# Seven products of quarters for 19 of the 22 up pairs in both gated MLPs of a three-layer fp32 kernel

## The chip, the cores and the metric

One NeuronCore of a Trainium2 chip. The metric is the device time of one execution in microseconds. Three runs of the kernel before gave 1880.21, 1881.07 and 1881.81 us; the median is 1881.07 us.

## The reference, cut to what matters

The network has one block of a first type (pooling, stick-breaking attention, a plain MLP) and then two layers of a second type. The change lies in the gated MLP at the end of each second-type layer:

```python
h2 = _rmsnorm(x, g_ffn[l])                       # x: 512 positions x 1024
z = _dwconv(h2 @ w_up[l], w_dw_ffn[l], b_dw_ffn[l])   # w_up: 1024 x 5632, conv of 3 taps along the positions
zg, zv = jnp.split(z, 2, axis=-1)                # 2816 gate and 2816 value channels
x = x + (jax.nn.silu(zg) * zv) @ w_down[l]       # w_down: 2816 x 1024
```

Everything is float32, and the last layer is followed by one more rmsnorm.

## The kernel before, in words

Channels lie on partitions and the 512 positions on the free axis, so the stream `x` is eight tiles of 128x512. A product with weights takes a 128x128 block of weights as the stationary side and 512 positions as the moving side. To keep float32 accuracy each operand is split into a high and a low part (`fp32r`), and `mm3` (L378) issues three matmuls for a block: high with high (L380), high weights with low data (L381), low weights with high data (L382).

Weights come in units of up to eight blocks, in the order of use that `weight_plan` writes down. `prep` (L352) handles a unit: SP loads `raw` (L358, 512 KB, three buffers), ACT casts it to `whi` (L359), POOL subtracts to get `wlo` (L360); `whi` and `wlo` have four buffers each. `take` (L363) hands out one block after the other and prepares units up to three ahead of the one in use. SP, ACT and POOL work their queues in order; a scheduler laid the order down when the program was built.

The gated MLP of layer `l` is the last part of `layer2`. `norm_in` scales and splits `x` into `xh` and `xl` and sums squares into `acc`; `fin` (`finish` in `norm_in`) makes the factor `r` from them by a matmul with ones (`total`, L480) and `rsqrt`. As `r` is one number for each position it is applied after the product: first `proj_outer` computes four tiles (two pairs of gate and value) with `x`'s eight tiles in the outer loop, then `fin` runs, then come the other pairs, one tile after the other. A pair is a gate tile and a value tile of 128 channels; 22 pairs make the layer. Of each tile `conv3` multiplies by `r` (L1289, DVE), applies the middle tap (L1292, ACT) and the outer taps (L1293 and L1294, DVE); `silu` (L344), the product with the value (L1308) and `split` (L448 and L449) follow. After eleven pairs comes a chunk of `w_down`: eight output tiles of eleven blocks each, added to `x` (L1313). There are two such chunks in a layer. At the very end `final` computes the last two output tiles in halves of 256 positions, so that the norm and the outputs of the first half can run beside the second.

PSUM has eight banks here, all under the name `b`.

Of the kernel before, what the change touches and what calls it, by code (L numbers as in the profile page):

```python
# [21 lines left out]
P = 128  # L22
# [21 lines left out]
NCV = 4  # L44
FF2 = 2816
NF2 = FF2 // P
CHUNK2 = 11
GLU_EARLY = 3
NYB = 7
YBANKS = ("s", "s", "t", "t", "av")  # L50
# [25 lines left out]

def _span(c0, n=P):
    return np.arange(c0, c0 + n)


def weight_plan():
# [47 lines left out]
    for l in range(NL):  # L129
        cr = QL + KVL  # L130
        ca, cg = cr + ROPE, cr + ROPE + 512
        add(outer("w_in_2", l, KT, [_span(ca), _span(cg), _span(ca + P), _span(cg + P)]))
        for i in range(2, GLU_EARLY):
            add(tiles("w_in_2", l, k8, _span(ca + P * i)))
            add(tiles("w_in_2", l, k8, _span(cg + P * i)))
        add(tiles("w_in_2", l, k8, np.concatenate([cr + np.arange(32)] * 2 + [cr + perm] * 2)))
        for j in range(2):
            add(tiles("w_in_2", l, k8, _span(QL + P * j)))
        for j in range(3):
            add(tiles("w_in_2", l, k8, _span(P * j)))  # L140
# [20 lines left out]
        for c in range(NF2 // CHUNK2):  # L161
            fs = list(range(c * CHUNK2, (c + 1) * CHUNK2))
            if c == 0:
                add(outer("w_up_2", l, KT, [_span(P * f + o) for f in fs[:2] for o in (0, FF2)]))
                fs = fs[2:]
            for f in fs:
                add(tiles("w_up_2", l, k8, _span(P * f)))
                add(tiles("w_up_2", l, k8, _span(FF2 + P * f)))
            add([("w_down_2", l, P * k, _span(P * m)) for m in range(KT) for k in range(c * CHUNK2, (c + 1) * CHUNK2)])
    return units  # L170


def pack_weights(inputs, plan):
    out = np.zeros((len(plan), P, UNIT * P), np.float32)
    for u, blocks in enumerate(plan):
        for b, (name, l, r0, cols) in enumerate(blocks):
            w = inputs[name] if l is None else inputs[name][l]
# [4 lines left out]
    return out  # L182

# [66 lines left out]


class Kern:
    def __init__(self, tc, xT, w, vec, cst, pos, outT):
        self.tc, self.nc = tc, tc.nc
        self.xT, self.w, self.vec_d, self.cst_d, self.pos_d, self.outT = xT, w, vec, cst, pos, outT
        self.plan = weight_plan()
        self.units = {}
        self.prepped = 0  # L260
        self.cur, self.blk = 0, 0
        self.table, self.table_users = None, []
# [2 lines left out]
    def setup(self, ctx):  # L265
# [2 lines left out]
        pool = lambda name, bufs=1, **k: ctx.enter_context(tc.tile_pool(name=name, bufs=bufs, **k))  # L268
        self.const = pool("const")
        self.wp = pool("wp", 4, reuse_waits="tile")  # L270
        self.xp = pool("xp", KT, reuse_waits="tile")
        self.rp = pool("rp", 2, reuse_waits="tile")
        c = self.const
# [13 lines left out]
        self.tk = c.tile([P, S], F32, name="tk")  # L287
        self.epst = c.tile([P, 1], F32, name="epst")
        nc.gpsimd.memset(self.epst, EPS)
        self.lna = {}  # L290
        for n in (D, 512, QL, KVL):
            t = c.tile([P, 1], F32, name=f"lna{n}")
# [54 lines left out]
        return ins  # L347


    def prep(self, u, eng=None):  # L350
        nc = self.nc
        n = len(self.plan[u]) * P  # L352
        raw = self.wp.tile([P, UNIT * P], F32, name="raw", bufs=3)
        hi = self.wp.tile([P, UNIT * P], FR, name="whi")
        lo = self.wp.tile([P, UNIT * P], FR, name="wlo")
        cuts = (0, n) if eng is None else (0, n // 2, n)
        for cs in map(slice, cuts, cuts[1:]):
            nc.sync.dma_start(out=raw[:, cs], in_=self.w[u, :, cs])  # L358
            nc.scalar.copy(out=hi[:, cs], in_=raw[:, cs])  # L359
            (eng or nc.gpsimd).tensor_tensor(out=lo[:, cs], in0=raw[:, cs], in1=hi[:, cs].bitcast(F32), op=ALU.subtract)  # L360
        self.units[u] = (hi, lo)

    def take(self, n=1, ahead=AHEAD):  # L363
# [38 lines left out]
    def proj_outer(self, pool, tag, acts, n, parts=WHOLE, between=None):  # L402
# [90 lines left out]
    def norm_in(self, pool, gname, l, on_pool=KT - 2):  # L493
# [14 lines left out]
        def finish(pp, tag):  # L508
            r = self.rp.tile([P, S], F32, name="r", bufs=1)
            self.rsqrt(r, self.total(pp, tag, acc)[0], D)  # L510
            return r

        return acts, split, finish

# [467 lines left out]
    def layer2(self, l, carry=None):  # L982
# [299 lines left out]
        xgp = xg.__enter__()  # L1282
        acts, split_in, fin = self.norm_in(xgp, "g_ffn_2", l)
        split_in()
        ffc = tc.tile_pool(name="ffc", bufs=CHUNK2, reuse_waits="tile")
        fp = ffc.__enter__()

        def conv3(ps, f, tag):
            V.tensor_tensor(out=ps, in0=ps, in1=r, op=ALU.mult)  # L1289
            w3 = self.v("w_dw_ffn_2", l, 3 * f, 3)  # L1290
# [6 lines left out]
        for c in range(NF2 // CHUNK2):  # L1297
            a = []
            pss = []
            if c == 0:  # L1300
                pss = self.proj_outer(pp, "b", acts, 4)
                r = fin(pp, "b")
            for f in range(c * CHUNK2, (c + 1) * CHUNK2):
                pg, pv = pss[2 * f : 2 * f + 2] if 2 * f < len(pss) else (self.proj(pp, "b", acts), self.proj(pp, "b", acts))
                cg = conv3(pg, f, "cg")
                cv = conv3(pv, NF2 + f, "cv")
                self.act(AF.Silu, out=cg, in_=cg)
                V.tensor_tensor(out=cg, in0=cg, in1=cv, op=ALU.mult)  # L1308
                a.append(self.split(fp, cg, ("ah", "al")))
            tail = 2 if l == NL - 1 and c == NF2 // CHUNK2 - 1 else 0  # L1310
            for m in range(KT - tail):
                ps = self.proj(pp, "b", a)
                V.tensor_tensor(out=self.x[m], in0=self.x[m], in1=ps, op=ALU.add)  # L1313
            if tail:
                self.final(pp, a)
        self._close(ffc)
        self._close(xg)
        self._close(pp_)

    def final(self, pp, a):  # L1320

# [14 lines left out]

        def half(j, ps, cs):
            i = KT - 2 + j
            V.tensor_tensor(out=self.x[i][:, cs], in0=self.x[i][:, cs], in1=ps, op=ALU.add)
            gain(i, cs, cs.start == 0 or j == 0)  # L1340

        def norm(cs):
            self.rsqrt(r[:, cs], self.total(pp, "b", acc[:, cs], *late)[0], D)
            late.clear()
            for j in range(0, KT, OUT_TILES):
                o = op.tile([P, OUT_TILES, S // 2], F32, name="o")
                for i in range(OUT_TILES):
                    (G if j + i in OUT_POOL else V).tensor_tensor(out=o[:, i, :], in0=self.x[j + i][:, cs], in1=r[:, cs], op=ALU.mult)
# [7 lines left out]
            norm(HALVES[1])  # L1356


def program(tc, xT, w, vec, cst, pos, outT):
    from contextlib import ExitStack  # L1360

    with ExitStack() as ctx:
        k = Kern(tc, xT, w, vec, cst, pos, outT)
        k.setup(ctx)
        carry = k.block1()
        for l in range(NL):
            k.layer2(l, carry)
# [3 lines left out]
def arrays(inputs):  # L1371
    inputs = {n: np.asarray(a) for n, a in inputs.items()}
    return {
        "xT": np.ascontiguousarray(inputs["x"][0].T),
        "w": pack_weights(inputs, weight_plan()),
        "vec": pack_vectors(inputs),
        "cst": shape_constants(),
        "pos": np.ascontiguousarray(inputs["positions_2"]),
# [12 lines left out]
```

## Time and profile before

| | |
|---|---|
| median of 3 runs | 1881.07 us |
| profiled execution, its own time | 1880.29 us |
| its span, first to last instruction | 1878.6 us |
| PE busy | 1839.2 us (98%) |
| POOL, ACT, DVE busy | 50%, 50%, 51% |
| mean granted TensorE clock | 0.998 of full speed |
| DMA traffic | 164.89 MB, mean 88 GB/s |

Times in the views are microseconds from the span's start. The matmuls are pipelined: the duration of one row overlaps the next, so the price of a matmul is the distance between two starts. PEld is the load of weights, which runs beside the matmuls.

### The profile page before, as it was taken

The numbers are of one execution on the slowest core, as the hardware profiler recorded it, in microseconds if no ns is written. First come the engines' busy times: TensorE is split into PE (matmuls) and PEld (weight loads), VectorE is DVE, ScalarE is ACT, GpSimd is POOL, SyncE is SP. The second block draws the span as 40 slices with busy tenths as digits, with TensorE's granted clock in tenths as the row PEclk, the third lists the DMA queues.
The fourth block names the chain that finished last, engine by engine and source line by source line (L and its number), as shares of the span: only waits on it lengthen the run. The fifth ranks groups of instructions, "written<-read, shape, count | busy, mean of one in ns | idle before, by whom it ended". The sixth has DMA issues, their size and how long they took to land.

```text
span 1878.6 us, 22097 instructions
## 1 busy us (share of the span) xinstructions
PE 1839.2 (98%) x8448; PEld 1495.8 (80%) x8448; DVE 958.1 (51%) x1420; ACT 946.3 (50%) x1442; POOL 938.4 (50%) x510
## 2 busy tenths in 40 slices
PE   8999999999999999999999999999999999999997
PEld 6877888888888888766888888888866788888886
DVE  4666552724022037997565225522898565405543
ACT  6766633643243347697554224433778554314442
POOL 5233444644444557866644444454966464444442
PEclk9999999999999999999999999999999999999999
DMA  5111223222222222200222222222210122222221
GB/s 188 68 57 62 79 101 135 93 94 101 92 99 98 94 90 71 98 29 21 94 106 95 97 101 91 101 101 90 91 51 23 64 99 101 101 91 101 100 91 56
DMA packets 48649, 164.89 MB, mean 88 GB/s; under 512 B 5536, under 2 KB 7584, under 8 KB 48544
## 3 DMA queue, kind: packets, MB, share of 16 engines
q1 hardware_dynamic: 46304, 160.34, 24.3%
q10 hardware_dynamic: 2240, 3.15, 0.5%
q8 instruction: 66, 1.08, 0.2%
q14 instruction: 39, 0.32, 0.1%
HBM read 161.37 MB, written 2.10 MB: 87 GB/s over the span
## 4 chain that ended last, share of the span: by engine, by line
PE 89%; DVE 6%; ACT 3%; issue 1%; POOL 1%; DMA 0%; SPq 0%; DVEq 0%; ACTq 0%; POOLq 0%
PE b L381 23%; PE b L382 23%; PE b L380 23%; PE mm L381 3%; PE s L1140 3%; PE mm L380 3%; PE mm L382 3%; PE t L1157 2%; DVE xl L452 1%; PE av L1162 1%; PE av L1163 1%; PE cv L480 1%; ACT whi L359 1%; DVE x L650 1%; PE b L480 1%
## 5 line engine op out<-in xcount | busy, mean ns | idle before, releaser
L360 POOL TENSOR_TENSOR wlo<-raw,whi 128x1024 fp32r<-128x1024 f32 x300 | 720.9, 2405 | 809.9 <-ACT whi L359 809.6
L359 ACT CAST whi<-raw 128x1024 fp32r<-128x1024 f32 (+1 forms) x302 | 313.6, 1040 | 506.4 <-PE b L381 414.6
L380 PE MATMUL b<-xh,whi 128*128 128x512 f32 (+1 forms) x1296 | 495.4, 382 | 2.7 <-ACT xh L451 2.7
L381 PE MATMUL b<-xl,whi 128*128 128x512 f32 (+1 forms) x1296 | 491.4, 379 | 3.4 <-DVE xl L452 3.4
L382 PE MATMUL b<-xh,wlo 128*128 128x512 f32 (+1 forms) x1296 | 491.1, 379 | 0.0
L381 PEld LDWEIGHTS b<-xl,whi 128*128 128x128 f32 x1296 | 244.1, 188 | 51.9 <-DVE xl L452 4.2
L380 PEld LDWEIGHTS b<-xh,whi 128*128 128x128 f32 x1296 | 244.2, 188 | 50.5 <-ACT xh L451 3.1
L382 PEld LDWEIGHTS b<-xh,wlo 128*128 128x128 f32 x1296 | 244.1, 188 | 45.6
L380 PE MATMUL b<-ah,whi 128*128 128x512 f32 (+1 forms) x646 | 243.6, 377 | 0.0
L381 PE MATMUL b<-al,whi 128*128 128x512 f32 (+1 forms) x646 | 243.2, 377 | 0.0
L382 PE MATMUL b<-ah,wlo 128*128 128x512 f32 (+1 forms) x646 | 243.2, 376 | 0.0
L381 PEld LDWEIGHTS b<-al,whi 128*128 128x128 f32 x646 | 121.6, 188 | 22.4
L380 PEld LDWEIGHTS b<-ah,whi 128*128 128x128 f32 x646 | 121.5, 188 | 22.4
L382 PEld LDWEIGHTS b<-ah,wlo 128*128 128x128 f32 x646 | 121.6, 188 | 22.0
L1228 POOL TENSOR_TENSOR cacc<-cacc,pd 128x510 f32<-128x510 f32 (+14 forms) x94 | 119.8, 1275 | 26.6 <-ACT pd L1226 22.8
L1212 DVE SCALAR_TENSOR_TENSOR cv<-u,vec,cv 128x497 f32<-128x497 f32 (+13 forms) x146 | 108.2, 741 | 8.4 <-ACT cv L1202 6.5
L1289 DVE TENSOR_TENSOR b<-b,r 128x512 f32<-128x512 f32 x88 | 61.0, 697 | 97.3 <-PE b L382 97.1
L1313 DVE TENSOR_TENSOR x<-x,b 128x512 f32<-128x512 f32 x30 | 20.6, 687 | 161.3 <-PE b L382 161.3
L448 ACT CAST ah<-cg 128x512 fp32r<-128x512 f32 x44 | 27.3, 621 | 98.7 <-DVE cg L1308 98.7
L380 PE MATMUL mm<-xh,whi 128*128 128x512 f32 x176 | 69.3, 394 | 0.0
L871 DVE TENSOR_TENSOR b<-rl,b 128x512 f32<-128x512 f32 x32 | 22.1, 696 | 92.5 <-ACT rl L870 92.5
L381 PE MATMUL mm<-xl,whi 128*128 128x512 f32 x176 | 68.7, 391 | 0.0
(430 smaller groups left out, 2851.0 us busy)
## 6 DMA issues: line engine op xcount, KB each, us to landing
raw<-w SPq DMA_DIRECT2D x295, 512.0 KB, 3.2
x<-xT SPq DMA_DIRECT2D x8, 256.0 KB, 6.5
x<-xT ACTq DMA_DIRECT2D x8, 256.0 KB, 4.8
raw<-w SPq DMA_DIRECT2D x7, 256.0 KB, 2.6
outT<-o ACTq DMA_DIRECT2D x4, 256.0 KB, 2.4
outT<-o SPq DMA_DIRECT2D x4, 256.0 KB, 2.5
vec<-vec SPq DMA_DIRECT2D x1, 363.0 KB, 6.9
f<-pos SPq DMA_DIRECT2D x1, 256.0 KB, 3.3
```

Of the source, the lines that this page charges most:

```text
L359: nc.scalar.copy(out=hi[:, cs], in_=raw[:, cs])
L360: (eng or nc.gpsimd).tensor_tensor(out=lo[:, cs], in0=raw[:, cs], in1=hi[:, cs].bitcast(F32), op=ALU.subtract)
L380: mm(ps, lhsT=wb[0], rhs=xb[0], start=start, stop=False, **kw)
L381: mm(ps, lhsT=wb[0], rhs=xb[1], start=False, stop=False, **kw)
L382: mm(ps, lhsT=wb[1], rhs=xb[0], start=False, stop=stop, **kw)
L448: nc.scalar.copy(out=hi, in_=src)
L480: self.nc.tensor.matmul(full[:, :n], lhsT=self.ones, rhs=a, start=i == 0, stop=i == len(parts) - 1)
L1140: mm(s, lhsT=q[:, qb * P : (qb + 1) * P], rhs=k, start=True, stop=True)
L1157: nc.tensor.transpose(pt[:, qb * P : (qb + 1) * P], probs[qb][:, t * P : (t + 1) * P], self.ident)
L1212: ins = V.scalar_tensor_tensor(out=acc[:, o], in0=us[i][:, u], scalar=self.v("w_dw_conv_2", l, i * CONV_K + k), in1=acc[:, o], op0=ALU.mul ...
L1228: G.tensor_tensor(out=acc[:, o], in0=acc[:, o], in1=pd, op=ALU.add)
L1289: V.tensor_tensor(out=ps, in0=ps, in1=r, op=ALU.mult)
```

## The change

19 of the 22 pairs of each layer (`PLAIN2 = 3` stay as they were) are computed as a product of 2x2 quarters with seven multiplications in place of eight. The weights of a pair are cut into gate and value, and into the lower and upper half of the 1024 inputs (`a11`, `a12`, `a21`, `a22`, each four blocks); the data into the lower and upper half of the inputs and the left and right 256 positions (`B11`, `B21`, `B22` and four sums `T1` to `T4`). The seven products take the stationary sides `a11`, `a12`, `a22` and four sums of quarters, `S1` to `S4`. Each product is four blocks by 256 positions, three matmuls a block.

The sums of weights are made on the chip, in DRAM: `sums` lists for each layer 20 copies (issued on ACT's queue) and 20 accumulating transfers (issued on POOL's queue), each over up to four pairs (1 MB). `prep` issues one of these 80 behind every second weight unit from unit 26 on, with none between units 106 and 140: layer 0's 40 stand behind units 26 to 104 (the first block), layer 1's behind units 142 to 220 (the gated MLP of layer 0, units 141 to 235). `quarter_inputs` makes the seven data operands, high and low, from `x` and the norm's factor; therefore `fin` now stands inside `proj_outer`, behind its third step of eight. In these MLPs raw weights have five buffers and are loaded five units ahead. The down products come in three chunks (7, 7 and 8 pairs), the first three tiles of each with the pairs in the outer loop. In `final` the outputs of the first half are issued after the second half's factor, some of them behind the second half's last addition.

```diff
-CHUNK2 = 11
+CHUNKS2 = (0, 7, 14, 22)
+PLAIN2 = 3
+OUTER2 = 2
+NDOWN = 3
+SUM_PAIRS = 4
+SIDE = {u: 1 for u in range(26, 240, 2) if not 105 < u < 141}
+RAW2, LOAD_AHEAD2 = 5, 5
...
+        for _ in range(SIDE.get(u, 0)):
+            if self.side:
+                begin, on_pool = self.side.popleft()
+                self.issue_behind(begin(), rest if on_pool else cast)
...
+        def copy(dst, src):
+            return lambda: nc.scalar.dma_start(out=dst, in_=src)
+        def add(dst, src):
+            return lambda: nc.gpsimd.dma_start(out=dst, in_=src, accum_op=ALU.add, max_dma_last_dim=row)
...
+        for name, base, more in (("S1", "a21", "a22"), ("S3", "a11", "a21"), ("S2", "S1", "a11"), ("S4", "S2", "a12")):
...
+            stages += [(copies, "S1", l), [(adds, "S1", l), (copies, "S3", l)], [(adds, "S3", l), (copies, "S2", l)], (adds, "S2", l), (copies, "S4", l), (adds, "S4", l)]
...
+        while self.loaded < min(self.cur + 1 + self.load_ahead, len(self.plan)):
+            self.load(self.loaded)
...
             for k, a in enumerate(acts):
+                if k == OUTER_LAG + 2 and between is not None:
+                    between()
...
+                def snap(ps):
+                    t = fp.tile([P, S // 2], F32, name="snap", bufs=4)
+                    with tc.high_priority():
+                        A.copy(out=t, in_=ps)
+                    return t
+                def plus(out, a, b):
+                    with tc.high_priority():
+                        V.tensor_tensor(out=out, in0=a, in1=b, op=ALU.add)
+                def times(ps, name, start, stop):
+                    hi, lo = ops[name]
+                    for kk in range(KT // 2):
+                        self.mm3(ps, self.take(), (hi[:, kk], lo[:, kk]), start and kk == 0, stop and kk == KT // 2 - 1, skip_group_check=True)
+                def p4(g):
+                    times(g["v"][:, L], "T4", False, True)
+                    plus(g["v"][:, R], g["g"][:, R], g["u3"])
+                def p3(g):
+                    times(g["g"][:, R], "B22", False, True)
+                    plus(g["g"][:, R], g["g"][:, R], g["u2"])
+                    a.append(unit(g["f"], g["g"], g["v"], self.wneg[l][:, 3 * g["f"] : 3 * g["f"] + 3]))
...
+                    times(g["v"][:, L], "B11", True, False)
+                    u1 = snap(g["v"][:, L])
+                    times(g["g"][:, L], "B21", True, True)
+                    plus(g["g"][:, L], g["g"][:, L], u1)
+                    if old is not None:
+                        p4(old)
+                    times(g["v"][:, L], "T2", False, False)
+                    g["u2"] = snap(g["v"][:, L])
+                    times(g["g"][:, R], "T1", False, False)
+                    if old is not None:
+                        p3(old)
+                    times(g["v"][:, L], "T3", False, False)
+                    g["u3"] = snap(g["v"][:, L])
+                    old = g
```

How the instructions stand now. PE at the start of layer 0's MLP (`b` numbered 7975 to 7978 are the first four tiles, `whi`/`wlo` the weights, `ones` the matrix of the norm's total); before, the total stood behind the last of the 96 matmuls of `proj_outer`:

```order
L507 MATMUL b_7978<-xh_7902,whi_7826 128x512
L508 MATMUL b_7978<-xl_7903,whi_7826 128x512
L509 MATMUL b_7978<-xh_7902,wlo_7827 128x512
L609 MATMUL b_8034<-acc_7897,ones_115 128x512
L507 MATMUL b_7975<-xh_7904,whi_7826 128x512
L508 MATMUL b_7975<-xl_7905,whi_7826 128x512
```

The total (L609) now stands behind 36 of these matmuls, with 60 behind it.

ACT in layer 0, in the second chunk of pairs (`snap` holds a copy of a half bank, `cv`, `cg` and `ah` belong to the pair that is being finished, `S2` is a sum in DRAM). Before, two casts and four other operations made a pair:

```order
L421 CAST whi_9209<-raw_9135 128x1024
L1472 COPY snap_9225<-b_9156 128x256
L1442 ACTIVATE cv_9264<-b_9065,vec_67,wneg0_124 128x512
L421 CAST whi_9242<-raw_9172 128x1024
L1442 ACTIVATE cg_9260<-b_9066,vec_67 128x512
L1472 COPY snap_9286<-b_9156 128x256
L421 CAST whi_9293<-raw_9206 128x1024
L1472 COPY snap_9309<-b_9288 128x256
L390 ACTIVATE b_9066<-cg_9260 128x512
L421 CAST whi_9327<-raw_9239 128x1024
L577 CAST ah_9270<-b_9066 128x512
L464 DMA S2_1_1_163<-S1_1_1_162 16x16384
```

Snaps, casts of weights and the finishing of a pair alternate now, and a copy in DRAM stands between them.

POOL in the same chunk, where before it had only the `wlo` of each unit:

```order
L467 DMA S3_1_0_160<-wq 512x512
L422 TENSOR_TENSOR wlo_9139<-raw_9067,whi_9138 128x1024
L422 TENSOR_TENSOR wlo_9176<-raw_9101,whi_9175 128x1024
L422 TENSOR_TENSOR wlo_9210<-raw_9135,whi_9209 128x1024
```

One accumulating transfer stands in this queue for every four units here; where the transfers of `S2` and `S4` are issued it is one for every two.

## Rows read from the trace of the kernel before

**Rows 1.** The page: chain that ended last, by engine.
```profile
PE 89%; DVE 6%; ACT 3%; issue 1%; POOL 1%; DMA 0%; SPq 0%; DVEq 0%; ACTq 0%; POOLq 0%
```
**Rows 2.** Busy time by stretch (engine: us busy, instructions; clock, DMA share, GB/s).
```profile
10.00:13.00 3.00, 3.00 (x15) 2.47 (x14) 0.97 (x2) 3.00 (x6) 1.98 (x1) 1.00 1.04 403
946.00:1062.00 116.00, 116.00 (x513) 95.84 (x512) 66.91 (x93) 53.79 (x69) 50.73 (x22) 1.00 0.28 96
```
**Rows 3.** PE in order of time (start, duration), down products, 512 positions wide.
```profile
1845.72 0.39 PE L382 MATMUL b<-ah,wlo 128*128 128x512 f32 x1
...
1850.48 0.39 PE L382 MATMUL b<-ah,wlo 128*128 128x512 f32 x1
```
**Rows 4.** The same right behind, 256 positions wide.
```profile
1850.71 0.28 PE L380 MATMUL b<-ah,whi 128*128 128x256 f32 x1
...
1859.58 0.28 PE L382 MATMUL b<-ah,wlo 128*128 128x256 f32 x1
```
**Rows 5.** Start of layer 0's MLP in order of time (PE, DVE, ACT, DVE).
```profile
923.73 0.39 PE L380 MATMUL b<-xh,whi 128*128 128x512 f32 x1
...
932.00 0.68 DVE L463 TENSOR_TENSOR acc<-acc,sq 128x512 f32<-128x512 f32 x1
...
946.55 0.69 ACT L344 ACTIVATE r<-b,epst 128x512 f32<-128x512 f32 x1
...
949.50 0.69 DVE L491 SCALAR_TENSOR_TENSOR r<-b,r 128x512 f32<-128x512 f32 x1
```
**Rows 6.** Groups by line, 946 to 1062 us: busy us, mean ns | idle before, releaser.
```profile
L360 POOL TENSOR_TENSOR wlo<-raw,whi 128x1024 fp32r<-128x1024 f32 x22 | 52.9, 2404 | 67.7 <-ACT whi L359 67.7
...
L359 ACT CAST whi<-raw 128x1024 fp32r<-128x1024 f32 x22 | 23.1, 1052 | 27.4 <-PE b L381 27.3
...
L1292 ACT ACTIVATE cg<-b,vec 128x512 f32<-128x512 f32 x11 | 8.5, 772 | 3.3 <-DVE b L1289 3.3
...
L1293 DVE SCALAR_TENSOR_TENSOR cg<-b,vec,cg 128x511 f32<-128x511 f32 x11 | 8.2, 745 | 6.2 <-ACT cg L1292 6.2
L449 DVE TENSOR_TENSOR al<-cg,ah 128x512 fp32r<-128x512 f32 x11 | 7.6, 690 | 5.5 <-ACT ah L448 5.5
L344 ACT ACTIVATE cg<-cg 128x512 f32<-128x512 f32 x11 | 6.9, 631 | 12.2 <-DVE cg L1294 12.2
L448 ACT CAST ah<-cg 128x512 fp32r<-128x512 f32 x11 | 6.8, 621 | 23.1 <-DVE cg L1308 23.1
```
**Rows 7.** ACT and DVE on 256 positions out of PSUM, in order of time.
```profile
334.82 0.46 ACT L824 ACTIVATE ol<-b,vec 128x256 f32<-128x256 f32 x1
...
1867.50 0.41 DVE L1339 TENSOR_TENSOR x<-x,b 128x256 f32<-128x256 f32 x1
...
1870.19 0.43 DVE L489 SCALAR_TENSOR_TENSOR b<-b,f 128x256 f32<-128x256 f32 x1 [2.29 <-ACT f L344]
```
**Rows 8.** POOL in order of time: three `wlo` in one piece.
```profile
932.00 7.64 POOL L360 TENSOR_TENSOR wlo<-raw,whi 128x1024 fp32r<-128x1024 f32 x3 [1.74 <-ACT whi L359]
```
**Rows 9.** The tile `raw`: SP's issuing instructions, ns min/median/max.
```profile
L358 SPq DMA_DIRECT2D raw<-w x302: 327/328/653, 1.7 to 1831.2; - x151
```
**Rows 10.** ACT's queue in order of time: issuing two outputs.
```profile
1865.39 1.67 ACTq L1350 DMA_DIRECT2D outT<-o  x2
```
**Rows 11.** DMA: queues (packets, MB, share of 16 engines) and issues (KB each, us to landing).
```profile
q1 hardware_dynamic: 46304, 160.34, 24.3%
q10 hardware_dynamic: 2240, 3.15, 0.5%
...
raw<-w SPq DMA_DIRECT2D x295, 512.0 KB, 3.2
```
**Rows 12.** The last product matmul on PE, in order of time.
```profile
1866.84 0.28 PE L382 MATMUL b<-ah,wlo 128*128 128x256 f32 x1
```

More of the change, by code (lines that the diff above doesn't have):

```diff
@@ L78, in _span, with chunks2 @@
     return np.arange(c0, c0 + n)
+def chunks2():
+    return [range(a, b) for a, b in zip(CHUNKS2, CHUNKS2[1:])]
 def weight_plan():
@@ L160, in weight_plan @@
             add(tiles("w_o_2", l, k8, _span(P * i)))
[L161 to L169, printed above, removed]
+        ffn = [("w_up_2", l, P * k, _span(P * f + o)) for k in range(KT) for f in range(OUTER2) for o in (0, FF2)]
+        ffn += [("w_up_2", l, P * k, _span(P * f + o)) for f in range(OUTER2, PLAIN2) for o in (0, FF2) for k in range(KT)]
+        for ks in chunks2():
+            quarter = lambda which, f: [(which, l, f, kk) for kk in range(KT // 2)]
+            before = None
+            for f in ks:
+                if f >= PLAIN2:
+                    ffn += quarter("a11", f) + quarter("a12", f)
+                    if before is not None:
+                        ffn += quarter("a22", before)
+                    ffn += quarter("S2", f) + quarter("S1", f)
+                    if before is not None:
+                        ffn += quarter("S4", before)
+                    ffn += quarter("S3", f)
+                    before = f
+            down = [("w_down_2", l, P * k, _span(P * m)) for k in ks for m in range(NDOWN)]
+            ffn += down[:4] + quarter("a22", before) + down[4:8] + quarter("S4", before) + down[8:]
+            ffn += [("w_down_2", l, P * k, _span(P * m)) for m in range(NDOWN, KT) for k in ks]
+        add(ffn)
     return units
@@ L176, in pack_weights @@
         for b, (name, l, r0, cols) in enumerate(blocks):
+            if name in QUARTERS + SUMS:
+                continue
             w = inputs[name] if l is None else inputs[name][l]
@@ L289, in setup @@
         nc.gpsimd.memset(self.epst, EPS)
+        self.wneg = {}
+        for l in range(NL):
+            t = c.tile([P, 3 * NF2], F32, name=f"wneg{l}")
+            nc.gpsimd.tensor_scalar(out=t, in0=self.v("w_dw_ffn_2", l, 3 * NF2, 3 * NF2), scalar1=-1.0, scalar2=None, op0=ALU.mult)
+            self.wneg[l] = t
         self.lna = {}
@@ L347, in act, with load @@
         return ins
+    def load(self, u, halves=False):
+        nc = self.nc
+        n = len(self.plan[u]) * P
+        pool, bufs = self.raw_from
+        raw = pool.tile([P, UNIT * P], F32, name="raw", bufs=bufs)
+        if any(b[0] in QUARTERS + SUMS for b in self.plan[u]):
+            parts = self.sources(u)
+        else:
+            cuts = (0, n // 2, n) if halves else (0, n)
+            parts = [(c0, c1, self.w[u, :, c0:c1]) for c0, c1 in zip(cuts, cuts[1:])]
+        for c0, c1, src in parts:
+            nc.sync.dma_start(out=raw[:, c0:c1], in_=src)
+        self.raws[u] = raw
+        self.loaded += 1
     def prep(self, u, eng=None):
@@ L352, in prep @@
         n = len(self.plan[u]) * P
-        raw = self.wp.tile([P, UNIT * P], F32, name="raw", bufs=3)
+        if u not in self.raws:
+            self.load(u, eng is not None)
+        raw = self.raws.pop(u)
         hi = self.wp.tile([P, UNIT * P], FR, name="whi")
@@ new lines, in sources @@
+    def sources(self, u):
+        out = []
+        for b, (name, l, f, kk) in enumerate(self.plan[u]):
+            if name in QUARTERS:
+                src = self.wq[l, QUARTERS.index(name), f - PLAIN2]
+            elif name in SUMS:
+                reg, i = divmod(f - PLAIN2, SUM_PAIRS)
+                src = self.sum_of[l, name, reg].rearrange("r (x c) -> (r x) c", c=KT // 2 * P)[i * P : (i + 1) * P]
+            else:
+                src = None
+            key = (name, f) if src is not None else None
+            if out and out[-1][0] == key:
+                out[-1][2] = b + 1
+            else:
+                out.append([key, b, b + 1, src, kk])
+        res = []
+        for key, b0, b1, src, k0 in out:
+            if key is None:
+                res.append((b0 * P, b1 * P, self.w[u, :, b0 * P : b1 * P]))
+            else:
+                res.append((b0 * P, b1 * P, src[:, k0 * P : (k0 + b1 - b0) * P]))
+        return res
@@ L506, in split, with finish @@
                 self.sq_add(acc[:, cs], x, i == 0, nc.gpsimd if i < on_pool else nc.vector)
-        def finish(pp, tag):
+        def finish(pp, tag, both=False):
             r = self.rp.tile([P, S], F32, name="r", bufs=1)
-            self.rsqrt(r, self.total(pp, tag, acc)[0], D)
-            return r
+            tot = self.total(pp, tag, acc)[0]
+            if not both:
+                self.rsqrt(r, tot, D)
+                return r
+            self.rsqrt(r, tot, D, tot)
+            nc.scalar.copy(out=r, in_=tot)
+            return r, tot
         return acts, split, finish
@@ L1295, in conv3, with unit @@
             return c
[L1297 to L1315, printed above, removed]
+        def unit(f, pg, pv, wv, in_psum=True):
+            cg = conv3(pg, self.v("w_dw_ffn_2", l, 3 * f, 3), f, "cg")
+            cv = conv3(pv, wv, NF2 + f, "cv")
+            to = pg if in_psum else cg
+            self.act(AF.Silu, out=to, in_=cg)
+            V.tensor_tensor(out=to, in0=to, in1=cv, op=ALU.mult)
+            return self.split(fp, to, ("ah", "al"))
```

158 lines of the change are left out of this document (145 added, 13 removed).

## The prediction

> **What bounds the kernel now.** I read the chain of waits first. PE holds 89% of it and no other engine over 6% [rows 1], so what counts is how long PE needs and where it waits. Then I read busy time by stretch inside layer 0's MLP: over 116 us PE is busy for all 116 at full clock, while DVE, ACT and POOL are busy for 67, 54 and 51 us and the DMA engines for 0.28 of the time [rows 2]. There the MLP costs what its matmuls cost. Then I read PE in order of time for the distance of two starts. From 1845.72 to 1850.48 us lie 21 steps of matmuls that are 512 positions wide: 4.76/21 = 0.2267 us each [rows 3]. From 1850.71 to 1859.58 us lie 74 steps that are 256 wide: 8.87/74 = 0.1199 us [rows 4]. Half the width costs 53% of the time, not 50%; this decides how much of the saving is left.
>
> **The matmuls.** A pair before is 16 blocks of three matmuls 512 wide: 48 x 0.2267 = 10.88 us. A pair after is 7 x 4 blocks of three matmuls 256 wide: 84 x 0.1199 = 10.07 us. The saving is 0.81 us a pair, over 19 pairs and two layers 38 x 0.81 = 30.8 us. In columns it would be an eighth, 1.36 us a pair. It would be nothing if a step took 10.88/84 = 0.1295 us. The three other pairs and the down products keep their matmuls; a third chunk of down products adds eight additions to `x` on DVE, beside PE.
>
> **The norm's total, moved forward.** It now stands behind 36 of the outer matmuls, so PE comes to it at 923.73 + 36 x 0.2267 = 931.9 us, but the sum of squares is ready only when the last addition ends, at 932.0 + 0.68 = 932.7 [rows 5]. PE waits 0.8 us plus a release, say 1.0; the 60 matmuls behind it, which could run, wait too. With the new copies in front on ACT's queue, each at 0.33 to 0.84 us [rows 9, 10], I take 1.5 us a layer, **+3.0** for both (0 to 6).
>
> **Making the seven operands.** From the factor's first step to its last DVE step took 946.55 to 950.2, 3.6 us [rows 5]. With the total done near 934 the factor is there near 937.6. DVE then has 24 steps of 512 elements up to the last operand that the first pair needs, at 0.69 to 0.75 us [rows 6] 17 us, until about 955. PE has 60 matmuls and the third pair (48) left, 108 x 0.2267 = 24.5 us, until 958.5. Cost nothing, with 3.5 us in hand; if the steps took a third longer, 3 us a layer.
>
> **Snaps.** A half bank is accumulated in three goes, and ACT must copy it before the next product goes into it. Between lie two other products, 2 x 12 x 0.1199 = 2.88 us. A snap is 0.46 us [rows 7], and with one cast (1.05) and one other operation (0.77) [rows 6] in front of it is 2.3 us: covered. ACT has per pair 3.5 casts, three snaps and four operations, 3.7 + 1.4 + 2.8 = 7.9 of 10.07 us; DVE 3 x 0.43 + 6 x 0.75 = 5.8 [rows 6, 7]. Zero; a third operation in front would cost up to 0.7 us a pair, 27 us in all, the upper end.
>
> **POOL's subtraction.** A unit of eight blocks now feeds PE for 24 x 0.1199 = 2.88 us instead of 24 x 0.2267 = 5.44. POOL needs 2.40 [rows 6], and 7.64/3 = 2.55 back to back [rows 8]. It fits, with 0.33 us left of each unit. In layer 0 the accumulating transfers are issued from the same queue, and `wlo` waits behind them. No row shows what such an issue costs. Bounds are 0.33 us [rows 9] and a whole POOL instruction of 2.4 [rows 6]; the nearest row is an issue on another engine's queue at 1.67/2 = 0.84 [rows 10]. Of the 20 in layer 0, nine fall into product stretches with four units each (1.3 us free) and six with two (0.66 us free); the others lie beside down products. At 0.84 that is 6 x 0.18, **+1**; at 2.4 it is 9 x 1.1 + 6 x 1.7, 20 us. The Trainium skill, "DMA: Bandwidth & Descriptors", section on latency, puts the first byte of a DMA whose descriptors GpSimd writes at about 1 us; by it the term would be 2 us.
>
> **Transfers.** A unit of 524 KB now is wanted every 2.88 us, 182 GB/s. The sixteen engines moved 403 GB/s when full [rows 2], so two units take 2.6 of 5.76 us, a share of 0.45 against 0.28 before. In layer 0 one copy or accumulation of 1 MB comes on top for every two units. Counted once per byte it takes another 2.6 us: 5.2 of 5.76, and it fits. Counted for each read and write (two for the copy, three for the accumulation, 2.5 in the mean) it takes 6.5, and the sum is 9.1. No row shows a transfer from DRAM to DRAM. I take it near the lower end, since the nearest row is the load's, and the sums of layer 1 are not read for 50 units. Raw weights have about 9 us in hand (five buffers of 2.88 us, less some 5 us until cast, 1.05, subtraction, 2.40 [rows 6], and an estimated 1.5 of queueing let go of one), against 3.2 us to land [rows 11]. **+3** for waits here (0, or up to 2 us in each of 30 slots, 61 us). In the first block a unit lasts 5.44 us, and both transfers fit even at the dear end (2.6 + 6.5 of 10.9 us). Zero.
>
> **End.** The last matmul's result was there at 1866.84 + 0.28 = 1867.1 us, and its addition to `x` began at 1867.5 [rows 7, 12], 0.4 us later, behind outputs of the first half and a sum. That goes, and outputs take DVE's idle 2.3 us behind it [rows 7]. Zero, within 0.4.
>
> **Sum**, against the profiled execution's own 1880.3 us (span 1878.6 and 1.7 around it): 1880.3 - 30.8 + 3.0 + 1 + 3 = 1856.5. That execution lay 0.8 us under the median, so **1857 us** in runs like those shown, 24 us or 1.3% faster.
>
> **Rivals.** *The transfers starve the weights (slower).* Mechanism: in layer 0 three queues have work at once, SP's weights, ACT's copies, POOL's accumulations. If they take even turns, the weights get a third of the engines where they need 0.45, and two units take 7.8 us to come instead of 5.76. It decides once a 1 MB transfer needs more than the 3.16 us that the weights leave, 1.2 times a load's price; then a backlog grows, POOL and ACT come to wait for an earlier transfer, and `wlo` and the casts stand behind that wait. All 30 slots would give 61 us; as it starts late and the down products drain it, I take two thirds, 1857 + 40 = 1897 us (1881 to 1918). For it: the 2.5 accesses a byte. Against: the slack of five units, and that in this trace one queue carries nearly everything, 24.3% to 0.5% [rows 11], so nothing was ever shared. The same page of the Trainium skill, section on queues and rings, says that a DMA engine takes the queues with work in turn, a packet each; no run here shows it yet. By that rule this rival holds as soon as the backlog does. Net slower needs 24 us lost, 12 of 30 slots.
>
> *POOL bounds layer 0.* An issue of 2.4 us gives 1856 + 20 = 1876 us, still faster. POOL would be full there, and PE would wait on `wlo`. Layer 1 would be clean.
>
> *The snaps are late in both layers.* 0.35 to 0.7 us a pair gives 1870 to 1884 us. For it: ACT is 78% full and works in order. Against: snaps and casts both follow PE's progress, so neither blocks long before the other.
>
> **Chances.** A measurement of this kernel tells about 0.2%, 3.8 us, from no change. Forecast (1849 to 1864) 0.58; POOL 0.08 (faster); snaps or part of the other waits 0.12, of it 0.05 faster and 0.07 about the same; starved weights 0.22, slower. Faster 0.71, same 0.07, slower 0.22. The range goes from 1849 (no wait at all) to 1890, which leaves out two thirds of the starved case, 0.15, and 0.03 below.
>
> **What would show it.** Right: 84 matmuls in 10.1 us per pair, PE without gaps in layer 1's pairs, under 2 us of waiting at each total; layer 1's MLP shorter by about 14 us, layer 0's by 10 to 14. Wrong: a step of 256 columns above 0.125 us; PE idle in front of B11 or T2 for `wlo` or a snap; issues on POOL over 1.3 us; raw weights landing after more than 9 us in layer 0, and layer 0's MLP longer than layer 1's by over 10 us.

## The result: 1.4% slower, and the profile after

The changed kernel took 1906.8 us (median of 4 runs, 1904.6 to 1911.9) against 1880.7 for the kernel before, a ratio of 1.0142 (95% interval 1.0121 to 1.0163). The forecast was 1857 us, the range ended at 1890: both missed. The rival of starved weights (1881 to 1918 us) had the sign and the size, but that is in part luck: its mechanism made only part of the loss, as the experiments show.

The profiled execution took 1911.9 us, the slowest of the four and 5 us above their median; its span is 1910.2 us, 31.6 us more than the one of before. Busy time by the four stretches (up to layer 0's MLP, that MLP, layer 1's attention part, layer 1's MLP with the end), in the columns of [rows 2], after:

```profile
24.00:935.70 911.70, 892.87 (x4203) 721.98 (x4202) 452.84 (x693) 483.63 (x783) 470.57 (x271) 0.99 0.44 131
935.70:1316.30 380.60, 355.60 (x2271) 323.85 (x2270) 183.24 (x264) 193.44 (x281) 269.52 (x130) 0.96 0.78 226
1316.30:1542.80 226.50, 222.63 (x935) 162.12 (x934) 165.83 (x271) 155.59 (x265) 144.17 (x95) 0.99 0.21 70
1542.80:1910.20 367.40, 346.72 (x2325) 319.64 (x2323) 193.85 (x285) 194.79 (x285) 240.13 (x106) 0.97 0.40 130
```
and the same stretches of before:
```profile
24.00:923.70 899.70, 880.27 (x4201) 720.44 (x4200) 454.27 (x692) 484.95 (x785) 452.14 (x251) 1.00 0.24 84
923.70:1283.70 360.00, 360.00 (x1588) 297.71 (x1587) 157.78 (x211) 143.15 (x180) 173.06 (x76) 1.00 0.28 98
1283.70:1505.70 222.00, 217.96 (x935) 161.47 (x934) 165.24 (x270) 155.49 (x265) 142.72 (x93) 1.00 0.18 63
1505.70:1878.60 372.90, 362.82 (x1659) 302.04 (x1657) 166.24 (x232) 145.00 (x186) 161.62 (x71) 0.99 0.26 92
```
The stretches differ by +12.0, +20.6, +4.5 and -5.5 us. Two things stand out. Time went where no matmul had been changed (first and third row). And in the MLPs PE now idles, 25 us in layer 0's, at a granted clock below 1. PE's waits in layer 0's MLP (engine, line, releaser: us in total, times, longest; before had none there):

```profile
PE b L507 <- ACT snap L1472: 15.5, 8, 4.6
PE b L507 <- DVE b L1477: 4.9, 1, 4.9
PE b L609 <- DVE acc L592: 2.7, 1, 2.7
```
**Transfers.** The page's queues, after, to be read beside [rows 11]:
```profile
q1 hardware_dynamic: 75104, 190.24, 29.3%
q0 software_dynamic: 20096, 39.85, 11.7%
q10 hardware_dynamic: 3520, 42.99, 6.1%
```
The share of the span for each MB is the price that the prediction lacked: 0.117 x 1910.2/39.85 = 5.6 us for an accumulated MB (q0), 2.7 for a copied one (q10), 2.9 for a loaded one (q1). An accumulation costs 1.9 loads, a copy 0.9, in the mean 1.4; the prediction's rival decided from 1.2. From 1075 to 1150 us, where layer 0's products and side transfers meet, the queues' shares and the landing times are, after:
```profile
q0 software_dynamic: 3118, 6.19, 45.2%
q1 hardware_dynamic: 5548, 11.43, 42.4%
q10 hardware_dynamic: 160, 4.98, 15.9%
...
raw<-S SPq DMA_DIRECT2D x18, 256.0 KB, 9.7
raw<-wq SPq DMA_DIRECT2D x14, 256.0 KB, 11.0
```
The shares add up to 103.5%, so the engines are full; q0 and q1 hold nearly even shares of time, and a raw weight lands after 10 to 11 us, not 3. The Trainium skill, "DMA: Bandwidth & Descriptors", section on queues, rings and completion order, says that an engine takes the queues with work in turn, a packet each. The shares of 45.2% and 42.4% are nearly even, but the counts, 3118 packets of q0 beside 5548 of q1, are not, so these rows do not show that rule. How PE comes to wait, the chain of waits there (start, us, what) tells, and below it ACT's row for an earlier cast:
```profile
1122.38 12.99 DMA raw<-S
...
1137.16 0.22 ACT whi L421
...
1138.00 0.38 ACT snap L1472
...
1138.42 0.58 PE b L507
```
```profile
1134.92 1.04 ACT L421 CAST whi<-raw 128x1024 fp32r<-128x1024 f32 x1 [4.89 <-DMA raw<-w]
```
The wait is booked on a snap, but ACT had stood for 4.89 us at a cast that had no raw weights, with everything behind it in its queue, that snap too.

**Where the products begin.** Layer 1 has no side transfers, and there PE waits for 8.3 us in the first pair and for 0.6 us in all others. Its clock goes to the lower level right behind. The stretch from the first product on in layer 0 and in layer 1, and the 243 us that follow in layer 1:
```profile
975.20:1000.00 24.80, 17.78 (x116) 17.08 (x115) 23.01 (x30) 13.95 (x22) 15.40 (x8) 0.79 0.44 133
1577.00:1600.00 23.00, 14.69 (x103) 14.16 (x102) 23.00 (x28) 13.21 (x21) 11.95 (x6) 0.78 0.32 110
1600.00:1843.00 243.00, 242.38 (x1750) 228.79 (x1749) 109.25 (x172) 133.10 (x193) 176.75 (x74) 1.00 0.49 157
```
A mean of 0.79 or 0.78 there is 10 us at 1.2 instead of 2.4 GHz. At 0.1166 us a product step (the mean of the steps without a gap at the full clock), 116 matmuls need 13.5 us and 103 need 12.0, so each of the two stretches lost 11 us. What PE waits for is seen best in order of time, at layer 0's first pair (POOL, DVE and ACT):
```profile
954.96 2.72 DVE L1554 SCALAR_TENSOR_TENSOR h<-x,vec,b 128x512 f32<-128x512 f32 x4 [2.41 <-ACT r L645]
...
977.80 1.73 POOL L1564 TENSOR_TENSOR B22l<-h,B22h 128x512 fp32r<-128x512 f32 x1
978.32 1.77 DVE L1564 TENSOR_TENSOR T1l<-t,T1h 128x512 fp32r<-128x512 f32 x1
980.01 0.68 DVE L1564 TENSOR_TENSOR T2l<-t,T2h 128x512 fp32r<-128x512 f32 x1
980.07 2.85 POOL L422 TENSOR_TENSOR wlo<-raw,whi 128x1024 fp32r<-128x1024 f32 x1 [0.54 <-ACT whi L421]
980.61 2.86 DVE L1564 TENSOR_TENSOR T3l<-t,T3h 128x512 fp32r<-128x512 f32 x1
...
984.72 0.78 ACT L1442 ACTIVATE cv<-b,vec 128x512 f32<-128x512 f32 x1 [3.49 <-DVE b L1466]
...
986.33 0.36 ACT L1472 COPY snap<-b 128x256 f32<-128x256 f32 x1
...
987.93 0.41 DVE L1477 TENSOR_TENSOR b<-b,snap 128x256 f32<-128x256 f32 x1
```
DVE's sum at 987.93 stands behind the operands, ACT's snaps behind convolution steps of the plain pairs that wait for DVE. And DVE's subtractions of two tiles in SBUF, 0.68 us alone, end about 0.55 us after the POOL step that began ahead of them: 977.80 + 1.73 = 979.53 and 978.32 + 1.77 = 980.09; 982.92 and 983.47. They don't run beside it. The Trainium skill, "SBUF — State Buffer", section on who interferes with whom, says that a DVE step with two inputs in SBUF and a GpSimd step that reads it lock each other out; these rows agree.

**Matmuls nobody touched.** PE in order of time, 27 steps of 512 columns in the first block, after:
```profile
379.62 0.39 PE L507 MATMUL b<-xh,whi 128*128 128x512 f32 x1
...
385.92 0.40 PE L507 MATMUL b<-xh,whi 128*128 128x512 f32 x1
```
6.30/27 = 0.2333 us, where before they took [rows 3]'s 0.2267. The down products kept 0.2267. What sets the two apart is the place in SBUF: the two new tap tiles take 288 bytes each, so the weights and all tiles on the left side lie 576 bytes higher, while `xh`, `xl`, `uh`, `ul`, `yh` and `yl` of the first block and the attention parts lie on the right side, unmoved. By this layout their distance to the weights was a multiple of 128 bytes; now 64 are left over. The traces carry no addresses: the distances here and below come from the sizes of the tiles, and the runs test them by shifting tiles.

### The profile page after: what moved, and what is told of

Its sections match the earlier page's. It is cut to its first block, busy times and chain, and to the rows that moved or that the text cites. A ratio compares the mean times of both kernels' runs of the same rounds, so it can differ in the third digit from the quotient of the medians.

```text
span 1910.2 us, 25887 instructions
## 1 busy us (share of the span) xinstructions
PE 1836.0 (96%) x9798; PEld 1542.1 (81%) x9798; DVE 1011.6 (53%) x1526; ACT 1045.5 (55%) x1640; POOL 1135.2 (59%) x622
## 3 DMA queue, kind: packets, MB, share of 16 engines
q0 software_dynamic: 20096, 39.85, 11.7%
## 4 chain that ended last, share of the span: by engine, by line
PE 80%; DVE 9%; DMA 4%; ACT 3%; POOL 2%; issue 2%; ACTq 0%; SPq 0%; DVEq 0%; POOLq 0%
PE b L507 20%; PE b L508 20%; PE b L509 20%; PE s L1275 3%; PE mm L508 3%; PE mm L507 3%; PE mm L509 3%; DMA raw<-wq 2%; DVE xl L581 2%; PE t L1292 2%; POOL wlo L422 1%; PE av L1297 1%; ACT whi L421 1%; PE av L1298 1%; PE cv L609 1%
## 5 line engine op out<-in xcount | busy, mean ns | idle before, releaser
L422 POOL TENSOR_TENSOR wlo<-raw,whi 128x1024 fp32r<-128x1024 f32 (+1 forms) x358 | 865.1, 2434 | 630.8 <-ACT whi L421 599.5
L421 ACT CAST whi<-raw 128x1024 fp32r<-128x1024 f32 (+1 forms) x360 | 372.6, 1038 | 495.2 <-PE b L508 337.2
L507 PE MATMUL b<-xh,whi 128*128 128x512 f32 (+1 forms) x688 | 262.9, 382 | 2.7 <-ACT xh L580 2.7
L508 PE MATMUL b<-xl,whi 128*128 128x512 f32 (+1 forms) x688 | 258.8, 376 | 4.6 <-DVE xl L581 4.5
L509 PE MATMUL b<-xh,wlo 128*128 128x512 f32 (+1 forms) x688 | 257.8, 375 | 0.0
L508 PEld LDWEIGHTS b<-xl,whi 128*128 128x128 f32 x688 | 130.5, 190 | 33.4 <-DVE xl L581 6.2
L507 PEld LDWEIGHTS b<-xh,whi 128*128 128x128 f32 x688 | 130.6, 190 | 30.3 <-ACT xh L580 3.1
L509 PEld LDWEIGHTS b<-xh,wlo 128*128 128x128 f32 x688 | 130.6, 190 | 25.1
L1477 DVE TENSOR_TENSOR b<-b,snap 128x256 f32<-128x256 f32 x114 | 48.8, 428 | 89.9 <-PE b L509 81.4
L509 PE MATMUL mm<-xh,wlo 128*128 128x512 f32 x176 | 69.5, 395 | 0.0
```

What stands on the lines that cost most here:

```text
L421: cast = nc.scalar.copy(out=hi[:, cs], in_=raw[:, cs])
L422: rest = (eng or nc.gpsimd).tensor_tensor(out=lo[:, cs], in0=raw[:, cs], in1=hi[:, cs].bitcast(F32), op=ALU.subtract)
L507: mm(ps, lhsT=wb[0], rhs=xb[0], start=start, stop=False, **kw)
L508: mm(ps, lhsT=wb[0], rhs=xb[1], start=False, stop=False, **kw)
L509: mm(ps, lhsT=wb[1], rhs=xb[0], start=False, stop=stop, **kw)
L1477: V.tensor_tensor(out=out, in0=a, in1=b, op=ALU.add)
```

## The experiments

Medians are of 4 runs unless given, with the ratio to the kernel before on the same chip. Each edit stands alone in the changed kernel unless the text says otherwise. Small differences need care: the product steps have two levels (last section), and the mean step of the one profiled execution of each kernel lay between 0.1153 and 0.1176 us at a distance of 64 bytes, which over 3192 steps is worth up to 7 us.

**1. Addresses.** The tap tiles made wider:
```diff
-            t = c.tile([P, 3 * NF2], F32, name=f"wneg{l}")
+            t = c.tile([P, P], F32, name=f"wneg{l}")[:, : 3 * NF2]
```


> The changed kernel with the two negated-tap tiles made 512 bytes wide each instead of 264, so that all tiles behind them move up by 448 bytes and the weights stand to the activations on the right side of SBUF as they did before. Theory A (a matmul 512 wide steps 0.0066 us slower when its moving operand and the next weights differ in their address by 64 bytes modulo 128): the steps with xh, xl, uh, ul, yh and yl go back from 0.2333 to 0.2267 us, layer 0's MLP starts near 924 us instead of 935.7, layer 1's attention part takes 222 us instead of 226.5, and the whole is 14 to 16 us shorter, 1891 us; if the 256-wide products, which stepped 0.1166 us at the 64-byte distance, also go back to before's 0.1199, that gives back up to 3192 x 0.0033 = 10.5 us, 1901 us. Rival B (something else slows these matmuls, the loads or the longer program): MLP start stays at 935.7, 1907 us.

1897.9 us, 1.0092 (1.0077 to 1.0107), 8.9 us less. Layer 0's MLP began at 926.9 us, the 512-wide steps averaged 0.2274. The products took the dear level, 35 steps in 4.20 us = 0.1200, in order of time:
```profile
1109.74 0.28 PE L509 MATMUL b<-B21h,wlo 128*128 128x256 f32 x1
...
1113.94 0.28 PE L508 MATMUL b<-T1l,whi 128*128 128x256 f32 x1
```
Theory A holds, with the give-back it named (1891 us without it, 1901 with). The mirror image, in the kernel before:
```diff
+        nc.gpsimd.memset(c.tile([P, 144], F32, name="gap"), 0.0)
```


> The kernel before with one unused 576-byte constant tile, so that its weights and left-side tiles lie where they lie in the changed kernel. Theory A (relative address): the 512-wide steps with xh, xl, uh, ul, yh and yl in the attention parts and the first block go to 0.2333 us, layer 0's MLP starts 12 us later, near 936 us, and the whole takes 1895 to 1897 us. Rival B: no change, 1881 us.

1892.3 us, 1.0062 (1.0045 to 1.0078): an unused tile alone costs 12 us, somewhat less than theory A's 14 to 16. The same 27 steps took 6.30 us there:
```profile
379.69 0.40 PE L381 MATMUL b<-xh,whi 128*128 128x512 f32 x1
...
385.99 0.39 PE L381 MATMUL b<-xh,whi 128*128 128x512 f32 x1
```
Then experiment 1 with the quarter tiles 64 bytes lower (one line more):
```diff
+        pool.tile([P, 16], F32, name="gap")
```


> The padded kernel with the quarter operands 64 bytes lower, so that they keep the distance of 64 bytes modulo 128 to the weights, and the 512-wide operands the distance 0. Theory A2 (the distance 0 is better for 512-wide matmuls, 64 for 256-wide ones): products step 0.116 to 0.118 us, 512-wide matmuls 0.2267, and the whole takes 1898 - 3192 x 0.0025 = 1887 to 1891 us. Rival (the 256-wide step depends on something else): 1898 us.

1892.6 us, 1.0062 (1.0047 to 1.0077), 14.2 us under the changed kernel and 1.6 above theory A2's range; the products averaged 0.1168 us. Of these two distances 512 columns go better at 0, 256 columns at 64.

**2. Transfers.** Layer 1's sums left out:
```diff
-                src = self.sum_of[l, name, reg].rearrange(...
+                src = self.sum_of[0, name, reg].rearrange(...
-        for l in range(NL):
+        for l in range(1):
             stages += ...
```


> The changed kernel without the 40 transfers for layer 1's sums; layer 1 reads layer 0's sums in their place, so the sums of layer 1 are left out of the computation. Theory T (the transfers between DRAM places delay the weights of layer 0's MLP): layer 0's MLP falls from 380.6 us to about layer 1's, 362 to 368 us, and the whole to 1889 to 1894 us. If the loss of layer 0 came from the operands' making alone: 1907 us.

1883.3 us (10 runs), 1.0014 (1.0005 to 1.0023), 23.4 us less, more than theory T's 13 to 18. In layer 0's MLP the waits of PE that are left are those of the first pair and the total:
```profile
PE b L507 <- DVE b L1477: 4.1, 1, 4.1
PE b L507 <- ACT snap L1472: 3.8, 1, 3.8
PE b L609 <- DVE acc L592: 0.4, 1, 0.4
```
Then all transfers issued, but small:
```diff
+        rows = lambda l, r: (r[1] - r[0]) * P * KT // 2 * P // row // (1 if l == 0 else 16)
-            return lambda: nc.scalar.dma_start(out=dst, in_=src)
+            return lambda: nc.scalar.dma_start(out=dst[:n], in_=src[:n])
```


> The changed kernel with all 40 transfers for layer 1's sums issued, but each of a sixteenth of its rows; layer 1 reads layer 0's sums, so fifteen sixteenths of its own sums are left out of the computation. Theory T (the bytes on the DMA engines): as without the transfers, 1889 to 1894 us. Rival (the issues on POOL and ACT and the waits of one issue for an earlier one cost it): near 1907 us, or at 20 POOL issues of 1.43 us with 9 of them beyond what POOL has free, 2 to 10 us above the run without the transfers.

1884.3 us (7 runs), 1.0024 (1.0013 to 1.0035), 1.0 us above the run without: the bytes cost, not the issues. Raw weights of 256 KB landed after 2.8 to 2.9 us in both runs. Then moved:
```diff
-SIDE = {u: 1 for u in range(26, 240, 2) if not 105 < u < 141}
+SIDE = {u: 1 for u in [*range(26, 113, 2), *range(113, 141), *range(236, 264)] if u < 113 or u % 3}
```


> The changed kernel with the transfers of layer 1's sums issued elsewhere: 44 of the 80 in the first block, 19 in layer 0's attention part, 17 in layer 1's, none beside an MLP of the second type. Theory T (the bytes cost where the MLP's weights need the engines): as without the transfers, 1883 to 1888 us. Rival (they cost the same wherever they run, or the attention parts pay for issues in front of their work): 1895 to 1907 us, with the attention parts longer by 5 us or more each.

1890.7 us, 1.0050 (1.0035 to 1.0065), 16.1 us less, between the two forecasts. Layer 0's MLP is then as without transfers; from total to total the two attention parts grew by 4.4 and 4.2 us over that run. Both theories had a part.

**3. Operands.** The loop over groups of blocks put inside each operand:
```diff
-        for k in range(0, KT // 2, 2):
...
-            put("B11", b11, G)
-            put("B21", b21, G)
+        for k in ks:
+            put(k, "B11", b[k][0], G)
+        for k in ks:
+            put(k, "B21", b[k][2], G)
```


> The changed kernel with the operands made by operand (B11 of all blocks, B21 of all, then T2, T1, T3, T4, B22) in place of by group of blocks; the same steps. Theory O (PE waits at the first T2 and T1, 2.1 + 5.3 us in layer 0 and 4.0 + 5.0 us in layer 1, since the second group's steps of 1.7 us stand behind all of the first group's, and the lowered clock behind these waits costs some 5 us a layer more): the waits fall under 2 us a layer and the whole by 15 to 28 us, 1879 to 1892 us. Rival (DVE is full through this stretch, so the waits move to T3 or T4): 1900 to 1907 us.

1899.4 us, 1.0101 (1.0084 to 1.0118): 7.4 us less, half of theory O's least and at the rival's lower end. In layer 1 the wait for DVE's sum fell from 4.6 to 0.7 us and the one for the snap stayed at 3.8; in layer 0 the sum still took 8.1.

**All three.**

> All three together: operands by operand, transfers moved out of the MLP, padding and the quarter operands 64 bytes lower. If the parts add up: 1907 - 23 (transfers) - 18 (addresses) - 20 (operands) = 1846 us, 1838 to 1858; faster than the kernel before by 1.2 to 2.2%. If they do not add (a wait covers another): 1860 to 1875 us.

1870.1 us, 0.9941 (0.9926 to 0.9956), faster than before. The single gains, 16.1 + 14.2 + 7.4 = 37.7, give 1869.1: they add up; the forecast had put each part too high (23, 18 and 20). What is left at the first pair, both layers alike, is the snap:
```profile
PE b L507 <- ACT snap L1472: 4.6, 2, 3.5
```
**4. The snap behind the plain pairs.** In the changed kernel, then in the one with all three, their steps written later:
```diff
+                    u1 = snap(g["v"][:, L])
...
+                    late()
```


> The changed kernel with one edit: the three plain pairs' own steps (factor, convolution, silu, cast) are written behind the three snaps of the first product pair instead of ahead of that pair. Theory S (PE waits at the first T2 because its snap stands on ACT's queue behind the plain pairs' convolutions, which wait for DVE, which still makes operands): the waits of 2.1 us (layer 0) and 4.0 us (layer 1) at the first T2 go, with some clock, 1895 to 1901 us; the waits at T1 (5.3 and 5.0 us, a sum on DVE behind the operand steps) may stay. If T1's waits go too: 1885 to 1892. Rival (the operands themselves are late): 1904 to 1909 us.

1905.3 us, 1.0131 (1.0113 to 1.0149): the rival's range.

> The same edit in the kernel with all three repairs (1870 us). Theory S: the waits left there, 3.8 and 3.7 us at the first T2 and 1.4 and 1.6 us at the first T4, go, with 5 us of lowered clock: 1853 to 1860 us, faster than the kernel before by 1.1 to 1.5%. Rival (the plain pairs then hold their PSUM banks longer and the second product pair waits for them): 1866 to 1874 us.

1866.0 us, 0.9924 (0.9909 to 0.9939). Neither tested the theory: ACT's queue had hardly moved, the scheduler still put convolution steps ahead of the snap, whose waits stayed at 4.7 us a layer. The gain of 4 us is about what the product steps give, 0.1155 us in place of 0.1172 in the run before, 5 to 6 us over 3192 steps. So the order was forced:
```diff
+            if f % NF2 < PLAIN2:
+                self.issue_behind(ins, queue["snap"])
...
+                            self.issue_behind(V.tensor_tensor(out=ps, in0=ps, in1=r, op=ALU.mult), queue["plus"])
```


> The kernel with all repairs and late plain pairs (1866 us), with the order on the queues now forced: a plain pair's convolution on ACT behind a snap of the first product pair, its product with the factor on DVE behind a sum of it. In the run before, the queue orders had hardly moved (the first snap still behind two convolution steps), so that run did not test theory S. Theory S: the waits of 3.8 + 1.5 us a layer at the first T2 and T4 go, and with them 5 to 7 us of lowered clock in both layers together: 1849 to 1856 us. Rival (the plain pairs, now later, hold the banks that the second product pair wants, or DVE is late for the first sum): 1860 to 1870 us.

1864.7 us, 0.9911 (0.9895 to 0.9928), the best, but in the rival's range and not in theory S's. The snap's waits fell to 0.5 us a layer and the lowered clock in the MLPs went altogether, so the queue order was the cause of the waits; a shorter wait for a sum on DVE came in their place. Layer 0's waits, and the stretch from the first product on in both layers:
```profile
PE b L507 <- DVE b L1482: 1.9, 1, 1.9
PE b L507 <- ACT snap L1477: 0.5, 1, 0.5
PE b L507 <- DVE cg L1446: 0.5, 1, 0.5
```
```profile
965.30:990.00 24.70, 24.01 (x199) 23.07 (x198) 24.70 (x38) 18.99 (x29) 22.71 (x8) 1.00 0.46 145
1537.70:1560.00 22.30, 21.33 (x176) 20.54 (x175) 22.30 (x36) 16.96 (x27) 21.13 (x7) 1.00 0.44 137
```
These stretches lost under 2 us each, where the changed kernel's lost 11. Against the run before it the gain of 1.3 us is within what can be told: more of the products ran at the slower of two levels (below), 0.1173 us a step in place of 0.1155, which is 5 to 6 us.

**5. More transfers early,** 22 of them in the first 190 us:
```diff
+SIDE = {u: 1 for u in [*range(4, 26), *range(26, 113, 2), *range(120, 141, 3), *range(240, 264, 3)]}
```


> The kernel with all repairs and late plain pairs, with 22 more of the 80 transfers issued in the first 190 us, one a unit, and only 14 in the two attention parts in place of 36. If transfers beside attention cost their 7 us there (the moved run stood 7 us above the run without them): 3 to 6 us below the run with the earlier placement. If the early ones delay the first weights instead: no gain, or up to 5 us slower.

1870.3 us, 0.9944 (0.9927 to 0.9960), 4.3 us above the run with late plain pairs: the second forecast. The first block took 9 us longer and layer 0's attention part 4 less, so that the MLP of layer 0 began at 935.7 us, not 930.4; layer 1's attention part got no shorter.

**6. Other distances,** the gap of the forced-order kernel at 24 and at 8 elements:

> The kernel with forced queue order (1865 us), its quarter operands at a distance of 32 bytes to the weights modulo 128 instead of 64. At 64 the 256-wide step shows two levels that each hold for hundreds of matmuls, 0.1133 and 0.1177 us; at distance 0 one, 0.1199. Theory A3 (the distance sets the step): a single level near 0.115 us, as the eight such steps of attention in the kernel before had, so 0 to 8 us less than 1865 where most of the products ran at 0.1177. Rival (the level is set by how PE entered the stretch, whatever the distance): again two levels, 1860 to 1866 us.

1866.4 us, 0.9925 (0.9911 to 0.9940). The products averaged 0.1180 us; two levels again, near 0.1173 and 0.1187 over 84 steps, each held for hundreds.

> The same at a distance of 96 bytes. Theory A3: a single level near 0.119 us, as the seven such steps in the kernel before had, 1867 to 1871 us. Rival: two levels, 1860 to 1866 us.

1867.8 us, 0.9932 (0.9916 to 0.9949), in theory A3's range. Single steps lay mostly from 0.115 to 0.123 us, but the mean over any 84 of them was from 0.1182 to 0.1186: one level, as at the distance 0. So theory A3 held at 96 bytes and failed at 32. What picks the level at 32 and at 64 stays open.

## Why the prediction was wrong, step by step

**The matmuls: the mechanism right, the saving better than said by luck.** The products averaged 0.1166 us a step, 84 x 0.1166 = 9.79 us a pair, so 38 pairs saved 41 us and not 30.8. The 0.1199 of the forecast is the step at the distance 0, where experiment 1 found it again; the shift of 64 bytes, which nobody had planned, made the products cheaper. The step that failed is one not written: that the other matmuls keep their 0.2267 us. The same shift cost them 14.2 us, with no work moved.

**The norm's total (+3.0): the sum of the waits right, by luck.** PE waited 2.7 us in layer 0 and 0.4 in layer 1, not 1.5 in each. In layer 0 the last addition of squares took 2.83 us and not 0.68, beside a subtraction on POOL, and behind the wait the clock was at 1.2 GHz for 6.8 us, which costs 3.4 more:
```profile
943.91 2.83 DVE L592 TENSOR_TENSOR acc<-acc,sq 128x512 f32<-128x512 f32 x1
```

**Making the seven operands ("cost nothing, with 3.5 us in hand"): wrong.** PE waited only 0.3 us for the first operands (B11, B21). Two things failed. The price of a step was 0.69 us only where POOL was idle, up to 2.9 beside POOL: up to T3, the last operand wanted before the second pair begins, DVE took from 954.96 to 983.47 us in layer 0, 28.5 us and not 17. And nothing else was asked of DVE and ACT until then: the pair's snaps and sums stand in the same queues, behind operands and plain pairs. PE waited there 6.8 us in layer 0 and 8.3 in layer 1, and the granted clock fell behind it for 10 us in each layer. That a stall also costs clock had no term. Together 22 us were lost where the forecast had zero. (Steps a third longer, 23 us in place of 17, would by the forecast's own figures have cost 2 us a layer, not 3.)

**Snaps (zero): right from the second pair on** (0.6 us in 243, in layer 1), wrong in the first. (The 0.7 us a pair for a third operation in front does not follow from the figures: 2.3 + 0.77 is 0.2 us over the 2.88 that cover it.)

**POOL's subtraction (+1): right.** Small transfers with all issues cost 1.0 us over none, below what a measurement tells; 20 us was the other bound. An issue held POOL for 1.0 us (median of 40), where 0.84 had been taken.

**Transfers (+3; 0 to 61): wrong, the largest failing step that one run isolates.** 23.4 us measured. The value was taken near the lower end because the load was the nearest row; an accumulation cost 1.9 loads. The rival's mechanism held in its main part, late raw weights, with about 23 of the 40 us it was given; that POOL and ACT wait for an earlier transfer is not shown, ACT waited for the weights themselves.

**The end (zero, within 0.4): off by 1.0.** From the last product matmul to the end of the span it was 1878.6 - 1866.84 = 11.8 us [rows 12]; after, 1910.2 - 1897.45 = 12.8. The wait for an addition went, and one for a square came in its place:
```profile
1897.45 0.28 PE L509 MATMUL b<-ah,wlo 128*128 128x256 f32 x1
...
1899.82 0.70 PE L609 MATMUL b<-sq,ones 128*128 128x256 f32 x2 [1.66 <-ACT sq L596]
```

Against the forecast the failing steps are thus the transfers (23 us in place of 3), the first pair of each layer (22 in place of 0) and the matmuls left as they were (14 in place of 0); the products gave 10 more than said.

The profiled difference can be put together too, as the time of each stretch less what its matmuls need at the steps above: -41 for the products; +16.5 in the two stretches outside the MLPs; 6 around the total of layer 0 and 1 around that of layer 1; 11 in each first pair; 24 in layer 0 from 1000 to 1311 us, and 2 in layer 1 from 1600 us on; 1 at the end: together about 32 against 31.6 measured. These are sums over one execution, an estimate; the runs above separate the causes.

## What to carry to other kernels

A change that adds a constant moves every tile behind it: compare the steps of matmuls that were not touched before explaining anything else. Price a transfer between two DRAM places from a trace of one, and put it where the loads leave the engines free, not where the change itself doubles their demand. Where work starts after a norm, ask of each engine's queue which small step PE needs first and what stands ahead of it; the cover of the large steps says nothing of that.

## What the hardware showed that was not expected

In these runs the step of a matmul depends on the distance of its moving operand to its weights in SBUF, counted here modulo 128 bytes (a weight shift of 576 changed it, one of 1024 did not; a longer period than 128 is not excluded). At 512 columns it was 0.2267 us at 0 and 0.2333 at 64; at 256 columns 0.1199 at 0, and at 64 one of two levels, 0.1133 or 0.1178, each of which holds for hundreds of matmuls. In the changed kernel, 27 steps in 3.06 us in layer 0, and in 3.18 us in layer 1:
```profile
999.84 0.28 PE L509 MATMUL b<-T1h,wlo 128*128 128x256 f32 x1
...
1002.90 0.28 PE L509 MATMUL b<-T3h,wlo 128*128 128x256 f32 x1
```
```profile
1689.81 0.28 PE L507 MATMUL b<-T1h,whi 128*128 128x256 f32 x1
...
1692.99 0.28 PE L507 MATMUL b<-B11h,whi 128*128 128x256 f32 x1
```
The share of the fast level was 26% in the changed kernel, about half in the kernel with all repairs and late plain pairs, and 11% with the order forced, in one execution each. With 3192 product steps, 0.0045 us between the levels is worth up to 14 us; nothing tried here sets it.
